# Weights, forms and normed operands placed earlier in the program in the four full units of a two-layer FP32 trunk

## The chip, the cores and the metric

The kernel runs on one core of one Trainium2 chip, as a single launch. The time is device microseconds (us) from the first to the last instruction as the chip measures it for an execution. Engines are named as the profile names them: PE is TensorE (matmuls; PEld are its weight loads), DVE is VectorE, ACT is ScalarE, POOL is GpSimd, SP is SyncE, which here does little but issue the loads.

## The reference

One inference step of a two-layer trunk with model width 1024, all in FP32. 512 columns are a new stream's prompt and 8 x 16 columns are the next frames of eight running streams, so T = 640 columns in all. Each layer has a mixer (layer 0: a gated MLP beside a gated short convolution; layer 1: forgetting attention) and then a convolutional feed-forward network (FFN), both with a residual:

```python
def _rmsnorm(x, g):
    xf = x.astype(jnp.float32)
    y = xf * lax.rsqrt(jnp.mean(xf * xf, axis=-1, keepdims=True) + EPS)
    return (y * g.astype(jnp.float32)).astype(x.dtype)
...
def _conv_ffn(x, prev, w_up, conv_w, w_down):
    z, st = _causal_dwconv(x @ w_up, conv_w, prev)
    gate, up = jnp.split(z, 2, axis=-1)
    return (jax.nn.silu(gate) * up) @ w_down, st
...
        hp = _rmsnorm(xp, norm_ffn[layer])
        hs = _rmsnorm(xs, norm_ffn[layer])
        zero_f = jnp.zeros((xp.shape[0], CONV_W - 1, 2 * D_FF), xp.dtype)
        yp, st_p = _conv_ffn(hp, zero_f, w_up[layer], conv_ffn[layer], w_down[layer])
        ys, st_s = _conv_ffn(hs, state_ffn[layer], w_up[layer], conv_ffn[layer], w_down[layer])
```

The up-projection goes from 1024 to 5632 channels, half of them gate and half up, and the down-projection from 2816 back to 1024. The last two up-projected columns of each stream are returned too (the new state of the convolution).

## The kernel before

**Tiles and precision.** The activations stand transposed, as eight tiles of 128 channels x 640 columns. TensorE multiplies a rounded FP32 form (fp32r), so each operand is split in a high and a low part and a product is the sum of three: high x high, high x low, low x high. A block of 128 output channels over 1024 inputs is 8 x 3 x 2 = 48 matmuls, each of a 128 x 128 weight tile with 320 columns (`mm`, L251). Splitting a 128 x 1024 weight block costs an ACT cast for the high part (`whi`) and then either a DVE subtract for the low part (`wlo`, function `weights`, L94 and L95), or, in `weights_added`, an ACT cast (L102), an ACT negation (L103) and a DMA that POOL issues and that adds the weights from memory onto the negated high part (L104). All loads of weights (`raw`) are issued by SP.

**The FFN.** The 5632 up-projected channels are 22 gate blocks and 22 up blocks. Gate block j and up block j make a unit. A unit's two blocks in PSUM are multiplied by the RMS factor of their columns (`rb`) into an SBUF tile with room for the convolution's history (`pad_evac`: DVE L340 and L341, and a small POOL copy L333). Then come the copy of the new state (ACT, L352), the convolution (ACT L346, DVE L348) of both blocks, SiLU (ACT L495), the product (DVE L498 and L499) and its split for the down-projection (ACT L135, DVE L136). The code calls what follows the eviction `act`.

**Full units and pair units.** Units 0 to 3 are full units: three products for each tile, with weights from `weights` in units 0 and 1 and from `weights_added` in units 2 and 3. From unit 4 on a unit is computed as a pair, gate and up over two halves of the rows and of the columns, by a scheme with seven products in place of eight (`pair_blocks`, matmuls on L201). It needs other operands:

- `forms(p)` makes, from channel tiles 2p and 2p+1 of x, two normed tiles `y` (DVE L152) and three sums and differences of their halves (DVE L156 to L159, 128 x 320 each), and splits these three (a cast and a subtract of 128 x 960, L135 and L136).
- `settle(p)` splits the normed tiles `y` into the tiles `hh` and `hl` in which the full units' operands stood (per tile an ACT cast and a DVE subtract of 128 x 640). It overwrites what the full units read.
- `pair_weights` loads both weight blocks, splits the gate block as it is (first part, up to its `yield`), then forms sums of the quarters (DVE L180) and splits these (second part).

From unit 4 on the down-projections of the four units before stand among the pair's products (`downs`; weights by `weights_down`, whose low part is again an adding DMA of POOL, `wlo<-w_dn`).

**What sets the order.** The program is written in Python and a scheduler of the framework arranges the instructions of each engine by its own estimate of times, with the order of the program as priority; once arranged, an engine runs its instructions strictly in that order. So where a call stands in the program decides which instruction gets in line first, and an instruction that waits holds up those behind it on its engine. Buffers limit how far ahead a weight can be prepared: four `raw` buffers (which the forms' sums use as well), five each of `whi` and `wlo`, eight pairs in the ring that holds the units' products and the forms' tiles `y`, and in PSUM three places of 128 x 1024 for the blocks, used in turn.

In the loop of `ffn` before the change, a unit is written as: load and split its weights and multiply (for unit 1 to 3 block by block), evict, copy the state, convolve and multiply, and last `forms(j)` for one pair of channel tiles. The next unit's weights come after all of this; and in unit 4 come, in this order, its weights' first part, a pair of down-projection weights, its weights' second part, `settle` for all four pairs, and the products.

Of the kernel before, what the change touches and what calls it, by code (L numbers as in the profile page):

```python
# [23 lines left out]
NJ = 22  # L24
PARTS = ((0, 4), (4, 8), (8, 12), (12, 16), (16, 20), (20, 22))
NSTD = 4
# [27 lines left out]
class Core:  # L54
# [28 lines left out]
    def weights(self, src, cols=1024, pieces=1, between=None):  # L83
        nc = self.nc
        raw = self.raw()
        hi = self.wp.tile([P, 1024], F32R, tag="whi", name=self.nm("whi"))
        lo = self.wp.tile([P, 1024], F32R, tag="wlo", name=self.nm("wlo"))
        n = cols // pieces
        for i in range(pieces):
            c = slice(i * n, i * n + n)  # L90
            if i == 1:
                between()
            nc.sync.dma_start(out=raw[:, c], in_=src[:, c])
            nc.scalar.copy(out=hi[:, c], in_=raw[:, c])  # L94
            nc.vector.tensor_tensor(out=lo[:, c], in0=raw[:, c], in1=hi[:, c].bitcast(F32), op=ALU.subtract)  # L95
        return hi, lo
# [36 lines left out]
    def part(self, hi, lo, src):  # L133
        nc = self.nc
        nc.scalar.copy(out=hi, in_=src)  # L135
        nc.vector.tensor_tensor(out=lo, in0=src, in1=hi.bitcast(F32), op=ALU.subtract)  # L136
# [345 lines left out]
    def ffn(self, l, x, h, g, rb, ring, fb, finish, out=None):  # L482


        nc, io = self.nc, self.io
        rpool, rtags = ring
        two = lambda a, n: a.rearrange("p (u c) -> p u c", u=2)

        def act(zg, zu, b):
            cvs = []  # L490
            for z, i in ((zu, 1), (zg, 0)):
                o = O_CF + (l * NB + b + i * NJ) * 3
                cv = self.conv(z, self.cst[:, o:o + 3])
                if i == 0:
                    nc.scalar.activation(out=cv[:, 0:CW], in_=cv[:, 0:CW], func=AF.Silu)  # L495
                cvs.append(self.conv_compact(cv))
            pr = self.tmp()
            nc.vector.tensor_tensor(out=pr[:, 0:TP], in0=cvs[1][0], in1=cvs[0][0], op=ALU.mult)  # L498
            nc.vector.tensor_tensor(out=pr[:, TP:T].rearrange("p (s c) -> p s c", c=16), in0=cvs[1][1], in1=cvs[0][1], op=ALU.mult)  # L499
            return self.split(rpool, rtags, pr[:, :T])  # L500

        def down(n, acts, ob, w):
            a, b = PARTS[n]
            ps = self.psum_d()
            for kc in range(b - a):
                self.mm((ps[:, C0:512], ps[:, 512:512 + HT]), w, kc, acts[kc], kc == 0, kc == b - a - 1)
            self.add_x(x[ob], ps)

        def downs(n, acts, ob):

            a, b = PARTS[n]
            w = self.weights_down(io["w_dn"][l, ob:ob + 2][:, :, a * P:b * P], (b - a) * P)
            return [lambda i=i: down(n, acts, ob + i, w[i]) for i in range(2)]

        forms, f, prev = [], None, None
        hk = [h[c] for c in KORD]
        first = [KORD.index(c) for c in range(NC)]
        zi = 0
        for n, (a, b) in enumerate(PARTS):
            si = self.fx.tile([P, 2, 64], F32, tag="si", name=self.nm("si"), bufs=2)  # L520
            so = self.fx.tile([P, 2, 72], F32, tag="so", name=self.nm("so"), bufs=2)
            nc.scalar.dma_start(out=si[:, :, 0:16 * (b - a)], in_=two(io["st_f"][l], NB)[:, :, 16 * a:16 * b])
            acts, left = [], [0, 2, 4, 6] if n else []
            for j in range(a, b):
                zg, zu = self.zp[zi % 3], self.zp[(zi + 1) % 3]
                zi += 2
                sts = [si[:, i, 16 * (j - a):16 * (j - a) + 16] for i in range(2)]
                if j < NSTD:
                    blocks = (j, NJ + j)
                    if j == 0:  # L530
                        ps = self.blocks([self.weights(io["w_up"][l, i]) for i in blocks], hk, first)
                    else:
                        weights = self.weights if j == 1 else self.weights_added
                        ps = [self.blocks([weights(io["w_up"][l, i])], hk)[0] for i in blocks]
                    for z, p_, st in zip((zg, zu), ps, sts):
                        self.pad_evac(z, p_[:, C0:C0 + T], rb, st)
                else:
                    w = self.pair_weights(io["w_up"][l, j], io["w_up"][l, NJ + j])
                    next(w)
                    dn = downs(n - 1, prev, left.pop(0))  # L540
                    w = next(w)
                    if f is None:
                        f = [self.settle(p, (h[2 * p], h[2 * p + 1]), forms[p]) for p in range(4)]
                    self.pair_blocks(w, f, zg, zu, sts, dn)
                for i, z in enumerate((zg, zu)):
                    self.new_state(z, so[:, i, 18 * (j - a):18 * (j - a) + 18])
                acts.append(act(zg, zu, j))
                if j < NSTD:
                    forms.append(self.forms(j, x, g, rb, ring, fb))
            for ob in left:  # L550
                for d in downs(n - 1, prev, ob):
                    d()
            nc.scalar.dma_start(out=two(io["o_sf"][l], NB)[:, :, 18 * a:18 * b], in_=so[:, :, 0:18 * (b - a)])
            prev = acts
        self.project([io["w_dn"][l, ob][:, a * P:b * P] for ob in range(8)], prev, None, x, finish, cols=(b - a) * P, out=out)
# [532 lines left out]
```

## Time and profile before

| | |
|---|---|
| median of 3 runs | 1645.4 us (1641.4, 1645.4, 1646.24) |
| profiled execution | 1644.36 us |
| its span, first to last instruction | 1642.6 us |
| mean granted TensorE clock | 0.949 |
| PE busy | 1485.1 us, 90% |
| DVE busy | 1055.4 us, 64% |
| ACT busy | 740.1 us, 45% |
| POOL busy | 207.8 us, 13% |

In a view of groups or of one engine's timeline, a row such as `L348 DVE SCALAR_TENSOR_TENSOR t<-zp,cst,t` is line 348 of the kernel on DVE, which writes tile `t` from tiles `zp`, `cst` and `t`; `x4` is the number of instructions in the row, and what stands in brackets is the idle time ahead of it with what ended that. The chain of waits lists, in order of time, start and duration of each piece of work that the next one waited for. The view of windows gives, for stretches of the span, the busy time of each engine with its number of instructions, the granted clock of TensorE (1.00 is full speed) and the share of DMA time. The part of the FFN from unit 0's last eviction to the first product of unit 4 lies at 229 to 349 us in layer 0 and at 1136 to 1256 us in layer 1.

### The profile page before, as it was taken

How to read it: one execution, taken by the hardware profiler on the slowest of the kernel's cores; microseconds unless marked ns; L12 is line 12 of the kernel's file. 1: busy time of each engine (PE TensorE's matmuls, PEld its weight loads, DVE VectorE, ACT ScalarE, POOL GpSimd, SP SyncE). 2: the span in 40 equal slices, each digit the busy share in tenths (PEclk: the TensorE clock that was granted, in tenths of full speed). 3: DMA queues.
4: the chain of work that ended last, by engine and by line, in shares of the span. 5: the costliest groups of instructions: out<-in, count | busy, mean ns of one | idle time of the engine just before them, and what ended most of it. 6: DMA issues, size and time to landing. Idle time of an engine off the chain costs nothing.

```text
span 1642.6 us, 26334 instructions
## 1 busy us (share of the span) xinstructions
PE 1485.1 (90%) x10576; PEld 1431.1 (87%) x10576; DVE 1055.4 (64%) x1805; ACT 740.1 (45%) x1326; POOL 207.8 (13%) x235
## 2 busy tenths in 40 slices
PE   8999965469999999999999999996546999999998
PEld 6999965459999999999989888886546999999998
DVE  6545442277777777677666667567327777877764
ACT  6322321255555555555544444344215555555551
POOL 4100210000101010126101010003000010101010
PEclk9999986779999999999999999998767999999999
DMA  7222102234444454443534424320223444544442
GB/s 249 84 78 65 39 21 60 66 92 103 114 110 121 103 126 103 98 160 111 173 110 133 133 87 170 91 76 26 77 66 88 107 107 105 129 105 120 103 95 87
DMA packets 74249, 168.04 MB, mean 102 GB/s; under 512 B 13760, under 2 KB 22896, under 8 KB 74000
## 3 DMA queue, kind: packets, MB, share of 16 engines
q1 hardware_dynamic: 49392, 133.79, 25.7%
q0 software_dynamic: 12032, 25.17, 9.5%
q10 hardware_dynamic: 12704, 7.41, 1.5%
q8 instruction: 83, 1.36, 0.4%
q14 instruction: 38, 0.31, 0.1%
HBM read 150.58 MB, written 11.54 MB: 99 GB/s over the span
## 4 chain that ended last, share of the span: by engine, by line
PE 86%; DVE 7%; DMA 2%; ACT 2%; issue 2%; POOL 0%; SPq 0%; DVEq 0%; ACTq 0%; POOLq 0%
PE mm L251 36%; PE zx L201 19%; PE pj L690 10%; PE aux L201 8%; PE po L251 2%; PE pv L766 2%; DMA wlo<-w_up 2%; DVE t L348 2%; PE pt L759 1%; DVE hl L282 1%; PE mm L389 1%; DVE wlo L95 1%; PE pt L845 1%; PE sc L752 1%; DVE y L152 1%
## 5 line engine op out<-in xcount | busy, mean ns | idle before, releaser
L135 ACT CAST sh<-raw 128x1024 fp32r<-128x1024 f32 (+2 forms) x152 | 142.4, 944 | 204.5 <-PE zx L201 101.9
L201 PE MATMUL zx<-hh,sh 128*128 128x320 f32 x576 | 179.9, 312 | 25.8 <-ACT sh L135 25.8
L251 PE MATMUL mm<-sh,wlo 128*128 128x320 f32 x872 | 201.4, 308 | 2.0 <-DMA wlo<-w_dn 2.0
L251 PE MATMUL mm<-sh,whi 128*128 128x320 f32 x872 | 200.6, 310 | 1.4 <-DVE x L359 0.9
L251 PE MATMUL mm<-hh,whi 128*128 128x320 f32 x512 | 125.6, 328 | 81.2 <-ACT whi L102 54.1
L251 PE MATMUL mm<-sl,whi 128*128 128x320 f32 x872 | 198.8, 309 | 0.0
L136 DVE TENSOR_TENSOR sl<-raw,sh 128x1024 fp32r<-128x1024 f32 (+2 forms) x152 | 164.8, 1092 | 38.9 <-ACT sh L135 32.7
L348 DVE SCALAR_TENSOR_TENSOR t<-zp,cst,t 128x656 f32<-128x656 f32 x184 | 162.9, 897 | 33.0 <-ACT t L346 31.9
L201 PE MATMUL zx<-hh,sl 128*128 128x320 f32 x576 | 179.0, 312 | 1.6 <-DVE sl L136 1.6
L201 PE MATMUL zx<-hl,sh 128*128 128x320 f32 x576 | 179.5, 312 | 0.0
L251 PEld LDWEIGHTS mm<-hh,whi 128*128 128x128 f32 x512 | 91.9, 202 | 82.9 <-ACT whi L102 55.2
L251 PEld LDWEIGHTS mm<-sh,whi 128*128 128x128 f32 x872 | 146.2, 188 | 2.8 <-DVE x L359 1.8
L251 PEld LDWEIGHTS mm<-sh,wlo 128*128 128x128 f32 x872 | 146.3, 188 | 2.6 <-DMA wlo<-w_dn 2.6
L251 PEld LDWEIGHTS mm<-sl,whi 128*128 128x128 f32 x872 | 146.1, 188 | 0.0
L251 PE MATMUL mm<-hh,wlo 128*128 128x320 f32 x512 | 120.5, 319 | 26.2 <-DMA wlo<-w_up 26.2
L94 ACT CAST whi<-raw 128x1024 fp32r<-128x1024 f32 (+3 forms) x94 | 79.9, 856 | 141.6 <-PE mm L251 85.8
L690 PE MATMUL pj<-whi,hl 128*128 128x256 f32 x480 | 137.3, 287 | 3.1 <-DVE hl L282 3.1
L359 DVE TENSOR_TENSOR x<-mm,x 128x640 f32<-128x640 f32 x111 | 91.2, 822 | 72.9 <-PE mm L251 72.6
L690 PE MATMUL pj<-wlo,hh 128*128 128x256 f32 x480 | 137.2, 286 | 0.0
L690 PE MATMUL pj<-whi,hh 128*128 128x256 f32 x480 | 136.7, 287 | 0.0
L201 PEld LDWEIGHTS zx<-hh,sh 128*128 128x128 f32 x576 | 109.9, 191 | 26.3 <-ACT sh L135 26.3
L251 PE MATMUL mm<-hl,whi 128*128 128x320 f32 x512 | 123.5, 324 | 0.3 <-DVE hl L282 0.3
(232 smaller groups left out, 3374.0 us busy)
## 6 DMA issues: line engine op xcount, KB each, us to landing
raw<-w_up SPq DMA_DIRECT2D x88, 512.0 KB
raw<-w_dn SPq DMA_DIRECT2D x40, 512.0 KB
wlo<-w_dn POOLq DMA_DIRECT2D x40, 512.0 KB, 5.9
raw<-w_c SPq DMA_DIRECT2D x24, 512.0 KB
raw<-w_ab SPq DMA_DIRECT2D x16, 512.0 KB
ck<-c_k SPq DMA_DIRECT2D x16, 512.0 KB
cv<-c_v SPq DMA_DIRECT2D x16, 512.0 KB
o_kv<-z ACTq DMA_DIRECT2D x8, 640.0 KB
```

The lines of the kernel that those rows point to most:

```text
L94: nc.scalar.copy(out=hi[:, c], in_=raw[:, c])
L95: nc.vector.tensor_tensor(out=lo[:, c], in0=raw[:, c], in1=hi[:, c].bitcast(F32), op=ALU.subtract)
L135: nc.scalar.copy(out=hi, in_=src)
L136: nc.vector.tensor_tensor(out=lo, in0=src, in1=hi.bitcast(F32), op=ALU.subtract)
L152: stt(out=y, in0=x[c], scalar=self.gv[:, 8 * g + c:8 * g + c + 1], in1=rb, op0=ALU.mult, op1=ALU.mult)
L201: nc.tensor.matmul(out, lhsT=l[:, c], rhs=r, start=start and p == 0 and i == 0, stop=p == 3 and i == 2, skip_group_check=True)
L251: nc.tensor.matmul(outs[h], lhsT=l, rhs=r[:, h * HT:(h + 1) * HT], start=start and k == 0, stop=stop and k == 2)
L282: nc.vector.scalar_tensor_tensor(out=lo, in0=x, scalar=gs, in1=hi.bitcast(F32), op0=ALU.mult, op1=ALU.subtract)
L348: nc.vector.scalar_tensor_tensor(out=cv[:, 0:CW], in0=zp[:, i:i + CW], scalar=w[:, i:i + 1], in1=cv[:, 0:CW], op0=ALU.mult, op1=ALU.add)
L359: self.nc.vector.tensor_tensor(out=x, in0=ps[:, C0:C0 + T], in1=x, op=ALU.add)
L690: nc.tensor.matmul(out[tb], lhsT=l[:, tb * P:(tb + 1) * P], rhs=r[:, c:c + 256], start=kc == 0 and i == 0, stop=kc == 7 and i == 2)
L766: nc.tensor.matmul(ov[64 * hh:64 * hh + 64, i * P:n], lhsT=z[2][:, j, (2 * pair + hh) * 64:(2 * pair + hh) * 64 + 64], rhs=u[:, j * P:(j + ...
```

## The change

In `ffn` the weights of unit j + 1 are now asked for right after the matmuls of unit j and ahead of its eviction, state copy and `act`; unit 0's are asked for ahead of the loop. In unit 3 the same place holds the first part of unit 4's pair weights and all four `settle`; the second part follows unit 3's evictions and stands ahead of its state copies. Unit 4's first pair of down-projection weights comes after that. The forms of pairs 0 and 1 now stand behind unit 0 and those of pairs 2 and 3 behind unit 1, where before each of the units 0 to 3 had one. The operations are the same as before; loads, casts, subtracts and adding DMAs move with the functions that contain them.

```diff
+        full = lambda j: [(self.weights if j < 2 else self.weights_added)(io["w_up"][l, i]) for i in (j, NJ + j)]
+        part = lambda j: self.pair_weights(io["w_up"][l, j], io["w_up"][l, NJ + j])
+        w = full(0)
         for n, (a, b) in enumerate(PARTS):
...
                 if j < NSTD:
-                    blocks = (j, NJ + j)
-                    if j == 0:
-                        ps = self.blocks([self.weights(io["w_up"][l, i]) for i in blocks], hk, first)
-                    else:
-                        weights = self.weights if j == 1 else self.weights_added
-                        ps = [self.blocks([weights(io["w_up"][l, i])], hk)[0] for i in blocks]
+                    ps = self.blocks(w, hk, first) if j == 0 else [self.blocks([v], hk)[0] for v in w]
+
+                    w = full(j + 1) if j + 1 < NSTD else part(j + 1)
+                    if j + 1 == NSTD:
+                        next(w)
+                        f = [self.settle(p, (h[2 * p], h[2 * p + 1]), forms[p]) for p in range(4)]
                     for z, p_, st in zip((zg, zu), ps, sts):
                         self.pad_evac(z, p_[:, C0:C0 + T], rb, st)
+                    if j + 1 == NSTD:
+                        w = next(w)
                 else:
-                    w = self.pair_weights(io["w_up"][l, j], io["w_up"][l, NJ + j])
-                    next(w)
-                    dn = downs(n - 1, prev, left.pop(0))
-                    w = next(w)
-                    if f is None:
-                        f = [self.settle(p, (h[2 * p], h[2 * p + 1]), forms[p]) for p in range(4)]
+                    if j == NSTD:
+                        dn = downs(n - 1, prev, left.pop(0))
+                    else:
+                        w = part(j)
+                        next(w)
+                        dn = downs(n - 1, prev, left.pop(0))
+                        w = next(w)
                     self.pair_blocks(w, f, zg, zu, sts, dn)
                 for i, z in enumerate((zg, zu)):
                     self.new_state(z, so[:, i, 18 * (j - a):18 * (j - a) + 18])
                 acts.append(act(zg, zu, j))
-                if j < NSTD:
-                    forms.append(self.forms(j, x, g, rb, ring, fb))
+                if j < 2:
+                    forms += [self.forms(p, x, g, rb, ring, fb) for p in (2 * j, 2 * j + 1)]
```

How this moves ACT's instructions is seen in layer 0, from unit 1's state copies on. Before, the rows are these; `sh` of 128 x 640 is the product of unit 1, `sh` of 128 x 960 the forms of pair 1, and the four rows at the end belong to unit 2's weights:

```order
L352 COPY so_2004<-zp_90 128x18
L352 COPY so_2004<-zp_88 128x18
L346 ACTIVATE t_2271<-zp_88,cst 128x656
L346 ACTIVATE t_2275<-zp_90,cst 128x656
L495 ACTIVATE t_2275<-t_2275 128x656
L135 CAST sh_2283<-t_2280 128x640
L135 CAST sh_2296<-raw_2291 128x960
L102 CAST whi_2302<-raw_2300 128x1024
L102 CAST whi_2358<-raw_2356 128x1024
L103 ACTIVATE wlo_2303<-whi_2302 128x1024
L103 ACTIVATE wlo_2359<-whi_2358 128x1024
```

In the changed kernel the same place has these; `whi_2278` to `wlo_2286` are unit 2's weights, and `sh_2161` and `sh_2174` the forms of pairs 0 and 1:

```order
L352 COPY so_2016<-zp_90 128x18
L102 CAST whi_2278<-raw_2276 128x1024
L352 COPY so_2016<-zp_88 128x18
L346 ACTIVATE t_2298<-zp_88,cst 128x656
L346 ACTIVATE t_2302<-zp_90,cst 128x656
L135 CAST sh_2161<-raw_2156 128x960
L103 ACTIVATE wlo_2279<-whi_2278 128x1024
L135 CAST sh_2174<-raw_2169 128x960
L102 CAST whi_2285<-raw_2283 128x1024
L103 ACTIVATE wlo_2286<-whi_2285 128x1024
L495 ACTIVATE t_2302<-t_2302 128x656
L135 CAST sh_2310<-t_2307 128x640
```

Unit 2's first cast went from behind unit 1's SiLU and product to between its state copies, and both negations now stand ahead of the SiLU, behind the conversion of pair 0's forms.

On DVE, the rows from unit 1's second eviction on, in the changed kernel, hold the end of the forms of pairs 0 and 1, interleaved, and then unit 1's convolution:

```order
L340 TENSOR_TENSOR zp_88<-mm_2227,rb_1974 128x512
L158 SCALAR_TENSOR_TENSOR raw_2156<-y_2153,y_2152 128x320
L341 TENSOR_TENSOR zp_88<-mm_2227,rb_1974 128x8x16
L158 SCALAR_TENSOR_TENSOR raw_2169<-y_2166,y_2165 128x320
L159 SCALAR_TENSOR_TENSOR raw_2156<-raw_2156,y_2153 128x320
L159 SCALAR_TENSOR_TENSOR raw_2169<-raw_2169,y_2166 128x320
L348 SCALAR_TENSOR_TENSOR t_2298<-zp_88,cst,t_2298 128x656
L348 SCALAR_TENSOR_TENSOR t_2302<-zp_90,cst,t_2302 128x656
```

Unit 1's subtracts for its low parts (L95), which stood behind unit 0's forms, are no longer ahead of this place on DVE: they went into the stretch before the FFN. In layer 1 that stretch reads on DVE as follows; L359 adds the mixer's output to x, L282 makes the normed low operands, and the two L95 rows are unit 1's:

```order
L359 TENSOR_TENSOR x_80<-mm_11657,x_80 128x640
L95 TENSOR_TENSOR wlo_11869<-raw_11867,whi_11868 128x1024
L95 TENSOR_TENSOR wlo_11875<-raw_11873,whi_11874 128x1024
L282 SCALAR_TENSOR_TENSOR hl_11645<-x_79,gv,hh_11644 128x640
L359 TENSOR_TENSOR x_81<-mm_11696,x_81 128x640
```

Before, the L282 row of `x_79` stood right behind the L359 row of `x_80`, with nothing between them.

## The prediction

> **What bounds the kernel now.** I read the slices of the page first, to see where PE is not full, then the waits of PE, then the windows of the stage in question, and last the chain of waits and the timelines of ACT and DVE inside it.
>
> ```profile
> PE   8999965469999999999999999996546999999998
> PEclk9999986779999999999999999998767999999999
> ```
>
> There are two dips, slices 6 to 8 and 28 to 30, one for each layer's full units, and the granted clock falls with them. PE's waits by releaser:
>
> ```profile
> PE mm L251 <- ACT whi L102: 54.1, 4, 13.5
> PE mm L251 <- ACT whi L94: 27.1, 2, 13.5
> PE mm L251 <- DMA wlo<-w_up: 26.2, 4, 7.7
> PE zx L201 <- ACT sh L135: 25.8, 2, 12.9
> ```
>
> (Total, times, longest, in us.) Together 133.2 us, 66.6 per layer: PE waits three times for the high part of the next unit's first weights (L94 for unit 1, L102 for units 2 and 3), after that in units 2 and 3 for the low part, and once for the operands of the first pair. Nothing else in the list is above 6 us. The windows from unit 0's last eviction to unit 4's first product, layer 0 and layer 1, and two stretches behind the first (duration, then busy time and instructions of PE, PEld, DVE, ACT, POOL, clock, DMA share, GB/s):
>
> ```profile
> 229.24:349.09 119.85, 53.11 (x290) 51.12 (x291) 53.76 (x82) 35.04 (x49) 7.97 (x15) 0.68 0.20 50
> 1136.22:1256.11 119.89, 51.88 (x291) 49.89 (x291) 53.77 (x82) 35.03 (x49) 7.31 (x12) 0.70 0.19 50
> 352.00:400.00 48.00, 45.99 (x307) 45.74 (x306) 35.80 (x51) 25.82 (x40) 4.66 (x6) 0.98 0.53 141
> 400.00:700.00 300.00, 300.00 (x2049) 300.00 (x2049) 222.21 (x321) 161.25 (x263) 33.32 (x47) 1.00 0.45 110
> ```
>
> In 119.85 us no engine is busy even half of the time, so this stage is bound by the chain through the engines. The last row gives the price of a matmul at full rate, 300.00/2049 = 0.146 us; a block (48) costs 7.05, a unit 14.1, and units 1 to 3 need 42.3 of the 119.85. The timeline of ACT shows the chain of one unit:
>
> ```profile
> 260.69 1.57 ACT L346 ACTIVATE t<-zp,cst 128x656 f32<-128x656 f32 x2
> 264.94 0.75 ACT L495 ACTIVATE t<-t 128x656 f32<-128x656 f32 x1 [2.67 <-DVE t L348]
> 266.65 0.72 ACT L135 CAST sh<-t 128x640 fp32r<-128x640 f32 x1 [0.96 <-DVE t L499]
> 271.16 0.99 ACT L135 CAST sh<-raw 128x960 fp32r<-128x960 f32 x1 [3.79 <-DVE raw L159]
> 272.06 1.99 ACT L102 CAST whi<-raw 128x1024 fp32r<-128x1024 f32 x2
> 273.95 2.00 ACT L103 ACTIVATE wlo<-whi 128x1024 fp32r<-128x1024 f32 x2
> ```
>
> Unit 2's cast at 272.06 needs only a loaded weight, but stands behind unit 1's convolution, SiLU, product and forms.
>
> **The change part by part.** Times t below count from 229.24, layer 0. DVE there, unit 0:
>
> ```profile
> 229.24 0.69 DVE L340 TENSOR_TENSOR zp<-mm,rb 128x512 f32<-128x512 f32 x1
> 229.85 0.28 DVE L341 TENSOR_TENSOR zp<-mm,rb 128x128 f32<-128x128 f32 x1
> 231.15 3.34 DVE L348 SCALAR_TENSOR_TENSOR t<-zp,cst,t 128x656 f32<-128x656 f32 x4 [1.02 <-ACT t L346]
> 235.91 0.28 DVE L499 TENSOR_TENSOR t<-t,t 128x128 f32<-128x128 f32 x1
> 236.99 0.83 DVE L136 TENSOR_TENSOR sl<-t,sh 128x640 fp32r<-128x640 f32 x1
> 237.73 0.88 DVE L152 SCALAR_TENSOR_TENSOR y<-x,gv,rb 128x640 f32<-128x640 f32 x1
> 238.64 0.49 DVE L156 TENSOR_TENSOR raw<-y,y 128x320 f32<-128x320 f32 x1
> 239.17 0.49 DVE L157 TENSOR_TENSOR y<-y 128x320 f32<-128x320 f32 x1
> 241.77 1.16 DVE L136 TENSOR_TENSOR sl<-raw,sh 128x960 fp32r<-128x960 f32 x1 [1.06 <-ACT sh L135]
> 242.84 2.35 DVE L95 TENSOR_TENSOR wlo<-raw,whi 128x1024 fp32r<-128x1024 f32 x2
> ```
>
> From start to start these give 0.9 for an eviction, 0.8 for an L152 or a 640 subtract, 0.52 for each of L156 to L159, 1.07 for a 960 subtract, 1.18 for an L95. The rows behind are the low-part DMAs on the chain of waits (start, duration), layer 0 and then 1, and the matmuls that follow the first:
>
> ```profile
> 275.34 5.66 DMA wlo<-w_up
> 312.11 7.39 DMA wlo<-w_up
> 1181.20 6.34 DMA wlo<-w_up
> 1217.75 7.99 DMA wlo<-w_up
> 281.05 15.39 PE mm L251 x88
> ```
>
> The mean landing is 6.85, and 88 matmuls after a pause cost 15.4 where full rate asks 12.9: 2.5 are the slow clock.
>
> *Unit 1.* Its weights are cast and subtracted ahead of the FFN, so PE runs from t 0 to 14.1. DVE ends unit 0's product at 6.95 (235.91 + 0.28 - 229.24), evicts unit 1's first block to 7.8, makes four L152 and a subtract (4.0) and four of the 0.52 us rows (2.1) to 13.9, and then evicts the second block, which is there at 14.1, to 15.0. Four more short rows end the two forms at 17.1.
>
> *Unit 2.* In ACT's new order `sh_2161` and then `wlo_2279` stand behind the two L346 (0.2 for L352 and 1.57: to 16.8). `sh_2161` ends at 17.7, `wlo_2279` at 18.6, its DMA lands at 25.5. Its `whi` is cast before that, so PE, after eight more matmuls (15.3), has one wait of about 10 here in place of two. The 88 matmuls that are then left end at 40.9.
>
> *Unit 3.* DVE goes on from 17.1: convolution 3.35 and two 960 subtracts 2.1 (22.6), SiLU 0.75 and product 0.9 (24.3), four L152 and a subtract (28.3), eight short rows (32.5). ACT converts both forms (34.5), then `wlo_2441` (35.4), which lands at 42.3; PE needs it four matmuls after 40.9, at 41.5, so about 0.8 is lost. New wait: the second block's cast `whi_2447` is queued behind L352, which waits for unit 2's first eviction, near 35; its low part lands at about 45 and is needed only at 48.6. Unit 3 ends at 56.0.
>
> *Pair start.* DVE's order puts unit 3's second eviction ahead of five of the eight settling subtracts, two other subtracts and an L180; from 56.0 these take 0.9 + 5 x 0.8 + 0.7 + 1.2 + 0.7 = 7.5, and the last operand is there at 63.5.
>
> ```profile
> L136 DVE TENSOR_TENSOR sl<-raw,sh 128x512 fp32r<-128x512 f32 x36 | 24.8, 690 | 18.9 <-ACT sh L135 12.9 <-PE aux L201 6.0
> L136 DVE TENSOR_TENSOR sl<-raw,sh 128x1024 fp32r<-128x1024 f32 x108 | 131.1, 1221 | 13.7 <-ACT sh L135 13.5
> wlo<-w_dn POOLq DMA_DIRECT2D x40, 512.0 KB, 5.9
> ```
>
> PE has about 54 products of ready operands among them, 54 x 0.146 = 7.9, so it can stay nearly covered, but the down-projection weights' accumulate (5.9 median) is now issued only behind the settling casts. I take 6 lost here in place of the 2.0 that row 352 to 400 shows lost (48.00 - 45.99), net 4; the bounds are 0 (all covered) and 9, nearly the last wait in the list above, 12.9 less some 4 of the settling that now comes early. The interval is then 56.0 + 4 = 60.0 and the gain 119.85 - 60.0 = 59.8. In layer 1 both of unit 2's casts stand behind the two L346, which adds two casts (2.0): 57.8.
>
> *Lead-in.* In layer 0 unit 1's weights go into a stretch with PE continuous and room on DVE. In layer 1 two L95 are put ahead of the L282 for which PE waits at the end of that stretch. Beside the adds of POOL they last longer than the 1.18 above:
>
> ```profile
> 1111.09 1.86 DVE L95 TENSOR_TENSOR wlo<-raw,whi 128x1024 fp32r<-128x1024 f32 x1
> 1114.99 2.59 DVE L95 TENSOR_TENSOR wlo<-raw,whi 128x1024 fp32r<-128x1024 f32 x1
> 1112.36 4.15 POOL L289 TENSOR_TENSOR acc<-acc,t 128x640 f32<-128x640 f32 x2 [0.48 <-ACT t L288]
> ```
>
> Two cost 2.4 to 5.2, or 0 where a wait for a matmul hides them; I take 3. The Trainium skill, page "SBUF — State Buffer", section "Who interferes with whom", says that a DVE instruction which reads two SBUF operands and a GpSimd instruction contend for one port, and that the loser stands fully blocked rather than slowed. The rows above agree in direction: 1.86 and 2.59 beside the adds. By that rule alone the pair could lose two whole adds on top of its own work, 2.4 + 4.15 = 6.5, and the sum would be 3.5 longer; the measured rows decide here.
>
> *Sum.* 59.8 + 57.8 - 3 = 114.6 against the profiled execution: 1644.4 - 114.6 = 1529.8. The median of the runs is 1.0 above that execution, so 1531.
>
> **The rivals.**
>
> *Waits vanish more fully, about 1509.* If unit 2's wait is halved (5 per layer, the forms done earlier) and the pair starts without a loss (6 per layer), 22 more are saved. For it: engines half idle in the window. Against: the low part of unit 2 is still behind one form and a DMA of 6.85. If PE never waited, 119.85 - 42.3 = 77.5 per layer would go, and 1489 is the floor.
>
> *DVE and DMAs slower, about 1557.* The window packs 54 us of DVE work into 60, with the DMAs of L104 among it:
>
> ```profile
> DMA to landing us min/median/max: 5.7/7.9/9.4
> ```
>
> If each of the four on the chain lands at the maximum, 9.4 in place of 6.85 (+10 in all), the pair start stays as dear as the 12.9 shown (7 above my 6, two layers: +14), and the lead-in costs 5.2 (+2), 26 come on top. For it: loads, forms and settling now coincide; against: the DMA share there was 0.20 and doubles to about 0.4 in half the time, less than the 0.53 of the row behind it.
>
> *The change does not do what it says, about 1645.* If the arranger had left unit 2's casts behind unit 1's forms and product, the chain above would stand. The order of ACT shown with the change speaks against it; in layer 1 the casts are behind the L346 alone.
>
> *Slower, about 1675.* The arranger plans the whole program anew. If its new order in the pair stage lets PE wait in each pair, as no wait does now (300.00 busy of 300.00), then with 36 pairs (the x36 row: one 512 split for each) the gain is gone at 114.6/36 = 3.2 us a pair; with 4 a pair, 144 are lost and the time is 1531 + 144 = 1675. For it: DVE is already at 222.21 of 300 there, and a subtract behind a late product would stall all. Against: no pair's code but the first is changed, and rows of the same kinds run in it.
>
> **How the numbers follow.** The forecast, 1512 to 1546, has 0.66; waits vanish more fully 0.12; slower DVE and DMAs 0.17; no effect 0.02; slower 0.03. The range 1504 to 1567 takes in the bounds: downward 8 for the pair starts, 3 for the lead-in and most of the second case; upward 10 for the pair starts, 2 for the lead-in, and the third case with some 10 beyond its time. A measurement of this kernel can tell about 0.3%, 4.9 us, from no change; by the cases, faster 0.95, the same 0.02, slower 0.03.
>
> **What would show it.** In the profile after, the two dips are shorter: the interval from unit 0's last eviction to the first L201 is 56 to 60 (layer 0), not 120. The waits for `whi` on L94 and L102 are nearly gone, those for `wlo<-w_up` come to 10 or 13 in unit 2 and under 2 in unit 3, and that for `sh` L135 is below 6 per layer. The lead-in of layer 1 grows by 2 to 5. If unit 2 begins much later than t 25, my reading of the queue on ACT is wrong; if the pair stage no longer shows PE at 300 of 300, the slower case is there.

## The result, and the profile after

The changed kernel takes 1528.5 us in the median (four runs, 1525.8 to 1532.7) against 1645.2 of the kernel before, a ratio of 0.930 (95% interval 0.927 to 0.932). That is 2.5 us below the forecast of 1531 and inside its narrower range. The profiled execution took 1525.84 us, with a span of 1524.0; the spans differ by 118.6 us where the sum had 114.6.

In the page of the changed kernel, the busy times and the slices of PE and of the granted clock show what is left of the two dips:

```profile
PE 1471.2 (97%) x10576; PEld 1418.3 (93%) x10576; DVE 1047.9 (69%) x1805; ACT 736.9 (48%) x1326; POOL 211.1 (14%) x235
...
PE   8999997899999999999999999999699999999998
...
PEclk9999998999999999999999999999899999999999
```

The number of instructions is that of before on every engine (10576, 1805, 1326, 235), and the busy times are within 14 us of it. What is gone is idle time. PE's waits by releaser, changed kernel:

```profile
PE mm L251 <- DMA wlo<-w_up: 10.9, 2, 8.0
PE mm L251 <- ACT whi L102: 10.4, 3, 6.2
...
PE mm L251 <- DMA wlo<-w_dn: 2.8, 1, 2.8
PE mm L251 <- DVE hl L282: 2.0, 1, 2.0
...
PE zx L201 <- ACT sh L135: 1.3, 1, 1.3
```

The four rows that stood for 133.2 us come to 22.6: L94 has left the list, L102 went from 54.1 to 10.4, the low parts from 26.2 to 10.9, and the first pair's operands from 25.8 to 1.3. The windows from unit 0's last eviction to the first of an unbroken row of pair products (layer 0, layer 1; busy times in the order PE, PEld, DVE, ACT, POOL, then clock, DMA share, GB/s), and then the longer stretch of layer 0 in which PE issues the 606 recorded matmuls that the stretch below it holds of the kernel before:

```profile
229.52:284.00 54.48, 45.41 (x288) 44.74 (x287) 44.40 (x71) 28.57 (x39) 9.62 (x13) 0.87 0.43 110
1075.76:1133.60 57.84, 45.67 (x283) 44.61 (x282) 45.63 (x74) 29.66 (x42) 8.26 (x10) 0.85 0.46 112
229.52:338.90 109.38, 94.92 (x606) 92.78 (x605) 87.91 (x134) 59.62 (x89) 15.51 (x22) 0.92 0.43 108
```

```profile
229.24:400.00 170.76, 102.02 (x606) 99.76 (x607) 92.40 (x135) 63.23 (x91) 12.75 (x21) 0.76 0.30 76
```

The interval fell from 119.85 to 54.48 us in layer 0 and from 119.89 to 57.84 in layer 1, that is by 65.4 and 62.1. Over the longer stretch layer 0 gains 170.76 - 109.38 = 61.4, so 4.0 of the 65.4 are given back when the pairs start. Counted from unit 0's last eviction to the start of attention's projections, 726.6 - 229.24 = 497.4 before and 665.5 - 229.52 = 436.0 after, the gain is 61.4 as well.

Inside unit 2 of layer 0, the matmuls of the changed kernel that waited, and the rows of ACT that they waited for:

```profile
250.33 0.90 PE L251 MATMUL mm<-hh,whi 128*128 128x320 f32 x2 [6.18 <-ACT whi L102]
254.66 0.90 PE L251 MATMUL mm<-hh,wlo 128*128 128x320 f32 x2 [2.90 <-DMA wlo<-w_up]
```

```profile
237.60 1.05 ACT L102 CAST whi<-raw 128x1024 fp32r<-128x1024 f32 x1
244.93 0.21 ACT L352 COPY so<-zp 128x18 f32<-128x18 f32 x1 [6.28 <-DVE zp L341]
245.04 1.57 ACT L346 ACTIVATE t<-zp,cst 128x656 f32<-128x656 f32 x2
246.52 0.98 ACT L135 CAST sh<-raw 128x960 fp32r<-128x960 f32 x1
247.40 1.05 ACT L103 ACTIVATE wlo<-whi 128x1024 fp32r<-128x1024 f32 x1
248.36 0.97 ACT L135 CAST sh<-raw 128x960 fp32r<-128x960 f32 x1
249.24 1.04 ACT L102 CAST whi<-raw 128x1024 fp32r<-128x1024 f32 x1
```

The first cast is done at 238.6. Its negation needs nothing else, but stands in line behind a state copy for which ACT idles 6.28 us, behind the convolution and behind pair 0's forms. So the wait in unit 2 is still one of order.

### The profile page after: what moved, and what is told of

Read it like the earlier page. It is cut to its first block, busy times and chain, and to the rows that moved or that the text cites. A ratio compares the mean times of both kernels' runs of the same rounds, so it can differ in the third digit from the quotient of the medians.

```text
span 1524.0 us, 26325 instructions
## 1 busy us (share of the span) xinstructions
PE 1471.2 (97%) x10576; PEld 1418.3 (93%) x10576; DVE 1047.9 (69%) x1805; ACT 736.9 (48%) x1326; POOL 211.1 (14%) x235
## 3 DMA queue, kind: packets, MB, share of 16 engines
q0 software_dynamic: 12032, 25.17, 10.4%
## 4 chain that ended last, share of the span: by engine, by line
PE 90%; DVE 3%; issue 2%; DMA 2%; ACT 2%; SPq 0%; POOL 0%; DVEq 0%; POOLq 0%
PE mm L251 37%; PE zx L201 20%; PE pj L696 11%; PE aux L201 8%; PE pv L772 3%; PE po L251 2%; PE pt L765 1%; DVE hl L282 1%; PE mm L389 1%; DVE wlo L95 1%; DMA wlo<-w_up 1%; PE pt L851 1%; PE sc L758 1%; PE sc L759 1%; PE scs L830 1%
## 5 line engine op out<-in xcount | busy, mean ns | idle before, releaser
L94 ACT CAST whi<-raw 128x1024 fp32r<-128x1024 f32 (+3 forms) x94 | 80.1, 856 | 149.6 <-PE mm L251 85.8
L359 DVE TENSOR_TENSOR x<-mm,x 128x640 f32<-128x640 f32 x111 | 91.2, 822 | 69.3 <-PE mm L251 69.0
L251 PE MATMUL mm<-hh,whi 128*128 128x320 f32 x512 | 120.3, 317 | 10.4 <-ACT whi L102 10.4
L251 PE MATMUL mm<-hh,wlo 128*128 128x320 f32 x512 | 118.5, 314 | 10.9 <-DMA wlo<-w_up 10.9
L251 PE MATMUL mm<-hl,whi 128*128 128x320 f32 x512 | 119.4, 315 | 2.0 <-DVE hl L282 2.0
L95 DVE TENSOR_TENSOR wlo<-raw,whi 128x1024 fp32r<-128x1024 f32 (+3 forms) x94 | 101.6, 1084 | 23.5 <-ACT whi L94 23.3
```

The source lines that it names most:

```text
L251: nc.tensor.matmul(outs[h], lhsT=l, rhs=r[:, h * HT:(h + 1) * HT], start=start and k == 0, stop=stop and k == 2)
L359: self.nc.vector.tensor_tensor(out=x, in0=ps[:, C0:C0 + T], in1=x, op=ALU.add)
```

## The experiments

The times are medians; the ratio is to the kernel before on the same chip. The changed kernel was run a second time beside the second group, with 1527.6 us, ratio 0.9281 (0.9266 to 0.9297).

| kernel | us | ratio, 95% interval |
|---|---|---|
| weights alone | 1549.2 | 0.9419 (0.9405 to 0.9434) |
| forms alone | 1574.0 | 0.9577 (0.9563 to 0.9591) |
| all but the pair's part | 1528.5 | 0.9297 (0.9280 to 0.9313) |
| subtract for the low parts of units 2 and 3 | 1516.3 | 0.9226 (0.9209 to 0.9242) |
| weights two units ahead | 1509.8 | 0.9171 (0.9157 to 0.9186) |
| both of these | 1510.1 | 0.9177 (0.9161 to 0.9193) |
| unit 1's low parts by DMA | 1523.9 | 0.9259 (0.9244 to 0.9273) |
| two ahead, one tap less | 1503.0 | 0.9146 (0.9133 to 0.9158) |
| two ahead, unit 1 by DMA | 1504.3 | 0.9156 (0.9143 to 0.9168) |

### The weights' part alone

```diff
-                    w = full(j + 1) if j + 1 < NSTD else part(j + 1)
-                    if j + 1 == NSTD:
-                        next(w)
-                        f = [self.settle(p, (h[2 * p], h[2 * p + 1]), forms[p]) for p in range(4)]
+                    w = full(j + 1) if j + 1 < NSTD else None
...
-                if j < 2:
-                    forms += [self.forms(p, x, g, rb, ring, fb) for p in (2 * j, 2 * j + 1)]
+                if j < NSTD:
+                    forms.append(self.forms(j, x, g, rb, ring, fb))
```

(Against the changed kernel; unit 4 is again as in the kernel before.)

> The weights' part of the change alone: the next full unit's weights ahead of a unit's evictions; forms again one pair behind each of units 0 to 3, unit 4's weights and the settling where they stood before. Theory (what kept PE waiting was the place of the next unit's casts behind the unit's chain and forms; the forms only matter in so far as they stand in unit 3 just ahead of the first pair): units 1 to 3 run as in the changed kernel, unit 2's low part lands at t 25 to 26 and unit 3 ends near t 55, but then the last form and the settling are all still to come and the pair waits about 13 us for sh (L135) as in the kernel before. Interval 55 + 14 = 69 in place of 119.85, gain 2 x 51 - 1 = 101: 1544 us (1536 to 1552). Rival (the weights are all of it, the forms cost nothing at the pair's start): 1528. Rival (two forms per unit are what shortens the chain, the weights follow from it): above 1590.

Measured: 1549.2, inside the theory's range and far from both rivals. PE's waits of this kernel:

```profile
PE zx L201 <- ACT sh L135: 28.9, 2, 14.4
PE mm L251 <- DMA wlo<-w_up: 12.2, 2, 6.3
PE mm L251 <- ACT whi L102: 5.7, 4, 2.4
```

The waits for weights are as short as in the changed kernel, 17.9 us, but the pair's wait for its operands is not shortened at all: 28.9, against 25.8 before. So the weights' place alone gives 1643.8 - 1549.2 = 95 us (against the kernel before on this chip), and most of what it leaves over is the pair's start.

### The forms' part alone

```diff
-                if j < NSTD:
-                    forms.append(self.forms(j, x, g, rb, ring, fb))
+                if j < 2:
+                    forms += [self.forms(p, x, g, rb, ring, fb) for p in (2 * j, 2 * j + 1)]
```

(Against the kernel before.)

> The forms' part alone: the kernel before with two pairs of forms behind unit 0 and two behind unit 1, none behind units 2 and 3; all weights where they stood before. Theory: units 1 and 2 still wait for casts behind the chain, now with two forms in it (some 3 us more each), but no form is left between unit 2 and unit 3 and between unit 3 and the pair: ACT's order has unit 3's casts right behind unit 2's, so unit 3's wait (13.5 + about 6) goes, and the pair's start loses about 8 less. Per layer 20 + 8 + 5 - 6 = 27 to 35, so 1575 to 1592 us. Rival (only the weights' place matters): 1640 to 1650. Rival (the forms are all of it): 1530.

Measured: 1574.0, a gain of 70 and 1 us past the better end of the theory's range. The matmuls of layer 0 that waited in this kernel, from unit 0 to the pair:

```profile
239.88 0.90 PE L251 MATMUL mm<-hh,whi 128*128 128x320 f32 x2 [8.75 <-ACT whi L94]
246.45 0.90 PE L251 MATMUL mm<-hh,wlo 128*128 128x320 f32 x2 [5.13 <-DVE wlo L95]
271.26 0.90 PE L251 MATMUL mm<-hh,whi 128*128 128x320 f32 x2 [8.75 <-ACT whi L102]
280.09 0.90 PE L251 MATMUL mm<-hh,whi 128*128 128x320 f32 x2 [7.40 <-ACT whi L102]
289.34 0.90 PE L251 MATMUL mm<-hh,wlo 128*128 128x320 f32 x2 [6.74 <-DMA wlo<-w_up]
```

Two waits for unit 1, three for unit 2, none for unit 3 and none for the pair's products: with no form behind unit 2, unit 3's casts stand right behind unit 2's, as expected. The two parts give 95 and 70 us alone and 117 together, so they overlap by 48. Unit 3's waits go with either of them and can go only once; in the kernel before they were 13.53 and 7.09 us in layer 0 and 13.53 and 7.70 in layer 1, which is 42 of the 48. Where the rest of the overlap lies stays open.

### The pair's part undone

```diff
-                    w = full(j + 1) if j + 1 < NSTD else part(j + 1)
-                    if j + 1 == NSTD:
-                        next(w)
-                        f = [self.settle(p, (h[2 * p], h[2 * p + 1]), forms[p]) for p in range(4)]
+                    w = full(j + 1) if j + 1 < NSTD else None
```

(Unit 4 is again as in the kernel before; weights and forms as in the changed kernel.)

> The changed kernel with the pair's part undone: weights early and forms two per unit, but the first pair's weights and the settling asked for in unit 4, behind the first down-projection weights, as before. The recorded step counted the earlier settling as a help at the pair's start (6 us lost there per layer where before it was 12.9). If that is right, undoing it costs up to 7 per layer: 1535 to 1542 us. Rival: the settling can start no earlier than the last read of the operands by unit 3 wherever it stands in the program, and the order of ACT and DVE hardly differs, except that the negation for wlo<-w_dn comes ahead of the settling again: then the wait for wlo<-w_dn (2.8 us in layer 0 of the changed kernel) goes, and it is 2 to 6 us faster than the changed kernel, 1523 to 1527.

Measured: 1528.5, the time of the changed kernel to 0.1 us. The help that the prediction saw in the earlier settling isn't there, and the 2 to 6 us of the rival aren't either. The rival's mechanism can be seen: the wait for `wlo<-w_dn` is no longer in the list of this kernel, but others have come in its place.

```profile
PE mm L251 <- ACT sh L135: 3.8, 3, 3.2
PE zx L201 <- DVE zp L341: 3.3, 2, 2.3
```

So at the pair's start it was the forms' move that helped, as it took two forms from behind units 2 and 3: the kernel with the weights alone differs from this one in the forms only, takes 1549.2, and waits 28.9 us there. Where the settling and the pair's weights stand in the program is worth nothing that these runs can tell.

### The low parts of units 2 and 3 by a subtract

```diff
-        full = lambda j: [(self.weights if j < 2 else self.weights_added)(io["w_up"][l, i]) for i in (j, NJ + j)]
+        full = lambda j: [self.weights(io["w_up"][l, i]) for i in (j, NJ + j)]
```

> The changed kernel with units 2 and 3 using the cast and DVE subtract of units 0 and 1 for their low parts in place of negation and adding DMA. Theory (what is left in unit 2 is the landing of the adding DMA, 5.8 in layer 0 and 8.2 in layer 1, behind the forms on ACT): the low part is there 1.2 us after DVE reaches it, right behind the forms, so the wait for wlo (2.9 in layer 0, 8.0 in layer 1) goes; but the second block's high part, for which PE waits first (6.2 in layer 0), stays behind the forms, and DVE has four subtracts of 1.2 more per layer. Net 5 to 9 us faster than the changed kernel: 1520 to 1524. Rival (DVE is the bound of this stage once PE's waits are short: 9.4 us more work on it show in full): 1536 to 1540.

Measured: 1516.3, 12 us faster than the changed kernel. The direction is the theory's, the size is not. In layer 0 one wait is left in unit 2:

```profile
247.24 0.90 PE L251 MATMUL mm<-hh,wlo 128*128 128x320 f32 x2 [3.13 <-DVE wlo L95]
```

The expectation kept the 6.18 us for the second block's high part. In layer 0 it is gone as well: by the order of PE's rows, the arranger now lets PE finish the first block before it turns to the second, where in the changed kernel it had interleaved the two, and PE stopped at a cast that it did not need yet. In layer 1 the wait of 7.98 for the low part is gone, and two waits for high parts are left, 3.63 and 0.80. The rival, that DVE's 9.4 us of added work would show, is out.

### Weights two units ahead

```diff
-        w = full(0)
+        ahead = [full(0), full(1)]
...
+                    w = ahead.pop(0)
                     ps = self.blocks(w, hk, first) if j == 0 else [self.blocks([v], hk)[0] for v in w]
-                    w = full(j + 1) if j + 1 < NSTD else part(j + 1)
+                    if j + 2 < NSTD:
+                        ahead.append(full(j + 2))
+                    if j + 1 == NSTD:
+                        w = part(j + 1)
```

(Beside it, on the same chip, the changed kernel once more.)

> The changed kernel unaltered, beside the three below on one chip, so that differences of a few us can be read: 1525 to 1532 us. No theory says otherwise.

> The changed kernel with the weights of the full units asked for two units ahead in place of one: units 0 and 1 ahead of the loop, unit 2's behind unit 0's matmuls, unit 3's behind unit 1's. In the arranged program all of unit 2's casts and negations come ahead of unit 0's evictions, so PE's wait in unit 2 (9.1 us in layer 0, 12.2 in layer 1) must go. Theory (with weights early, DVE is next: its work from unit 0's last eviction to the last settling subtract, laid end to end, was about 60 us in the working of the prediction, and PE has 42.3): the full units end near t 43 to 45, the saved time comes back in part as a wait of the first pairs for settled operands, and 3 to 8 us per layer are left: 1513 to 1523 us. Rival (DVE keeps up, PE's waits in unit 2 are simply gone): 1505 to 1508. Rival (the order's place of casts is not what holds unit 2): 1528.

Measured: 1527.6 for the changed kernel and 1509.8 for this one, 17.8 us faster; a little better than the theory's range and above the rival's. Its windows from unit 0's last eviction, layer 0 for the full units alone and then with the first pair:

```profile
229.68:273.90 44.22, 44.11 (x300) 43.62 (x298) 40.89 (x68) 24.98 (x38) 7.61 (x12) 1.00 0.37 88
229.68:290.00 60.32, 55.50 (x353) 54.26 (x352) 56.96 (x91) 35.20 (x53) 13.08 (x15) 0.92 0.38 100
```

The full units run without a gap, 44.11 of 44.22 us at clock 1.00, and the waits are behind them, at the pair:

```profile
275.27 0.41 PE L201 MATMUL zx<-hh,sh 128*128 128x320 f32 x1 [1.34 <-ACT sn L216]
277.05 0.63 PE L201 MATMUL zx<-hl,sh 128*128 128x320 f32 x1 [0.84 <-DVE hl L136]
282.61 0.63 PE L201 MATMUL aux<-sh,sl 128*128 128x320 f32 x1 [2.54 <-DVE sl L136]
```

DVE is busy 56.96 us of 60.32 here. That makes it the next bound by its busy time; whether its work sets the time is tried below, by taking some of it away.

### Two ahead and the subtract

The edits of the two last experiments together.

> As the run before (weights two units ahead), and the low parts of units 2 and 3 by a DVE subtract in place of negation and adding DMA. The subtract alone made the changed kernel 12 us faster, by taking away the DMA's landing. With the weights two units ahead that landing is hidden, and if DVE is the bound then, four subtracts of 1.2 us per layer, of which unit 2's two fall before the stage, cost 2 to 5 per layer: 4 to 10 us slower than the run before. Rival (the gains of the two edits add): 12 us faster than the run before.

Measured: 1510.1, the same as two units ahead alone. The gains do not add, which fits that both edits remove the same wait, that of unit 2. The loss of 4 to 10 us that the added subtracts were to cost does not show in the medians; the spans of the two profiled executions, 1509.5 and 1506.1, are 3.4 apart in its direction. So if there is a cost, it is at the low end or below what was expected, and the runs do not settle it.

### Two ahead and one tap less

```diff
-                cv = self.conv(z, self.cst[:, o:o + 3])
+                cv = self.conv(z, self.cst[:, o:o + 3], (1,) if b < NSTD else (1, 0))
```

(Against the kernel with weights two units ahead; `conv` is given the list of its DVE taps. This kernel leaves out a part of the convolution in the full units, so it returns other values and serves to measure only.)

> The kernel with weights two units ahead, with one of the two DVE taps of the convolution left out in the four full units (their convolutions have two taps in place of three; nothing else is left out). That takes two DVE instructions of 0.84 us from each unit, 6.7 us per layer, 5.0 of them ahead of the settling. Theory (with weights two ahead DVE is the bound: 56.96 us busy of the 60.32 from unit 0's last eviction on, in layer 0): 4 to 6 us per layer, 1498 to 1502 us. Rival (what is left at the first pair is the latency of the chain through ACT, POOL and DMAs, or the share of it that DVE sets is small): 1506 to 1510.

Measured: 1503.0, 1 us outside the theory's range and 3 from the rival's. By the ratios, 0.9146 against 0.9171, it gains 4 us, half of the least that the theory asked for the two layers together; the spans of the profiled executions are 7.5 us apart (1506.1 and 1498.6). From unit 0's last eviction to the start of attention's projections layer 0 gains 4.6 (657.7 - 229.68 = 428.0, and 652.3 - 228.88 = 423.4), nearly all of the 5.0 us of DVE work that was taken from ahead of the settling, so there the time follows DVE's work. Layer 1 gains only 2 us of 5. At its first pair PE's waits for DVE become shorter (2.66 to 1.18 for `sl`), but its wait for the cast `sh` grows from 2.26 to 3.42, and that cast stands on ACT behind the load of its weight; a wait of 1.71 for a down-projection weight comes in too. So DVE as the bound is shown for layer 0, by one profiled execution of each kernel, and not for layer 1.

### Unit 1's low parts by DMA

```diff
-        full = lambda j: [(self.weights if j < 2 else self.weights_added)(io["w_up"][l, i]) for i in (j, NJ + j)]
+        full = lambda j: [(self.weights if j < 1 else self.weights_added)(io["w_up"][l, i]) for i in (j, NJ + j)]
```

> The changed kernel with unit 1's low parts by negation and adding DMA in place of DVE's subtract, so that no subtract of unit 1 is ahead of the FFN on DVE any more. In the changed kernel the two subtracts took 4.48 us of DVE there in layer 1 and PE waited 2.0 for the next normed operand. Theory (the step of the prediction that charged 3 us for the lead-in, bounds 0 to 5.2, was too dear, since the next stop, the adds on POOL, is hardly later): 0.5 to 2 us faster than the changed kernel. Rival (blocked DVE time shows in full, as by the 6.5 us worked out beside the page): 4 to 6.5 us faster.

Measured: 1523.9, 3.7 us faster, between the two expectations. In the changed kernel DVE's lead-in of layer 1 reads

```profile
1057.22 0.81 DVE L359 TENSOR_TENSOR x<-mm,x 128x640 f32<-128x640 f32 x1
1057.95 4.56 DVE L95 TENSOR_TENSOR wlo<-raw,whi 128x1024 fp32r<-128x1024 f32 x2
1062.44 0.87 DVE L282 SCALAR_TENSOR_TENSOR hl<-x,gv,hh 128x640 fp32r<-128x640 f32 x1
```

and unit 0's evictions there began at 1075.15, without the two subtracts at 1072.80:

```profile
1075.15 1.29 DVE L340 TENSOR_TENSOR zp<-mm,rb 128x512 f32<-128x512 f32 x2 [3.83 <-ACT rb L325]
```

```profile
1072.80 1.29 DVE L340 TENSOR_TENSOR zp<-mm,rb 128x512 f32<-128x512 f32 x2 [3.83 <-ACT rb L325]
```

The first and last start of attention's first group of projections are the same in both, 665.5 and 951.3 in the changed kernel and 665.6 and 951.3 without the subtracts:

```profile
L696 PE MATMUL pj<-whi,hh x480: 277/283/387, 665.5 to 951.3; 128*128 128x256 f32 x160
```

```profile
L696 PE MATMUL pj<-whi,hh x480: 277/283/387, 665.6 to 951.3; 128*128 128x256 f32 x160
```

So the two cost 2.35 us of time for 4.56 of DVE. What the medians show beyond that, 1.3 us, is less than the spread of the runs. With the weights two units ahead, the same edit gives the fastest complete kernel of this study:

> The kernel with weights two units ahead, and unit 1's low parts by negation and adding DMA. Both edits alone made the changed kernel faster, by 18 and by 3.7 us. The second one acts ahead of the FFN of layer 1 (unit 0's evictions come 2.35 us earlier there), where the first one has changed nothing, so the gains should add: 1505 to 1508 us. Rival (four adding DMAs of 512 KB ahead of the stage in place of two arrive late, and unit 1 or 2 waits for them): 1510 to 1516.

Measured: 1504.3, just below the theory's range. The ratio is 0.9156 against 0.9171 with the subtracts, which is 2.5 us of the 3.7 that the edit gave alone, and the two intervals overlap. Of the profiled difference of 4.6 us, 3.2 come from ahead of layer 1's evictions. So the direction is that of gains that add, the size is not settled, and the rival's late DMAs did not come.

## Why the prediction was right, point by point

**The bound.** It was right that PE waited for casts that stood in line, and that the stage holds 42 us of PE work. Moving the weights alone brings 95 us.

**Unit 2.** The low part was to land at t 25.5 in layer 0 and 27.5 in layer 1. In the chain of waits of the changed kernel the two adding DMAs are

```profile
248.79 5.83 DMA wlo<-w_up
...
1095.43 8.16 DMA wlo<-w_up
```

and end at 254.62 - 229.52 = 25.1 and 1103.59 - 1075.76 = 27.8. The chain on ACT and DVE was laid end to end from single rows of the kernel before, and that held to within 1 us, since each engine runs its rows in the order shown. That the landings agree to 0.4 us is luck in part: the DMAs started at t 19.3 and 19.7, where 18.6 and 20.6 were worked out, and took 5.83 and 8.16, where the mean of 6.85 stood for both, so in each layer one error makes up for the other. What failed is a detail: PE was to do eight matmuls and then wait once for about 10 us. It did four, waited 6.18 for the second block's cast, which the order on ACT showed behind both forms, and then 2.90 for the low part: 9.1 in all.

**Unit 3.** 0.8 us were charged for its low part, and no wait is there. The second block's cast behind the state copy was a new wait in the program and cost nothing, as worked out.

**Pair start.** A net loss of 4 per layer was taken between bounds of 0 and 9: 4.0 in layer 0, and about the same in layer 1 (62.1 less the 58.1 gained there from unit 0's last eviction to the end: 118.6 - (1136.22 - 1075.76) = 58.1). In layer 0 the cause is the one named: PE waits 1.27 us for a cast and then 2.81 for the accumulate of the down-projection weights, whose negation stands behind settling casts. In layer 1 PE waits 3.08 at the same place. The number was right and one of its reasons was not: the prediction let the earlier settling help, and the kernel without it is as fast.

**Lead-in.** 3 us were charged, with bounds of 0 and 5.2. Against the kernel before, unit 0's last eviction came 0.6 us later, counted from the start of attention's projections (in the kernel before they start at 726.6: 1136.22 - 726.6 = 409.6, and 1075.76 - 665.5 = 410.3). The two subtracts do cost 2.35, as their removal shows, so the rest of the lead-in became 1.7 shorter; where that comes from stays open. The price of the two rows was at the lower end of the 2.4 to 5.2 worked out, and as a difference between the kernels the term was mis-sized.

**The sum.** Predicted 59.8 + 57.8 - 3 = 114.6, measured 61.4 + 58.1 - 0.6 - 0.3 = 118.6, where the last 0.3 is a later start of layer 0's stage. The lead-in is the largest difference. Layer 0's interval came out shorter than the sign of 56 to 60 said, 54.48. Two slips of the working do not bear on the result: 48 matmuls at 300.00/2049 are 7.03 us, not 7.05, and the floor of 1489 lacks the 1.0 that was added to the forecast for the median.

**The rivals.** Slower DMAs did not cost time: the two that PE waited for took 5.83 and 8.16 us, between 5.7 and 9.4. All eight landed a little later than before (median 8.3 after 7.9, at most 10.2), but PE did not wait for the other six. The case in which more of the waits vanish did not come with this change, as unit 2's wait of 9 to 12 us per layer stayed; asking for the weights two units ahead takes that wait away and reaches 1510. That the case had 1509 is chance, since it halved unit 2's wait and let the pair start without a loss, while here the whole wait is gone and the pair still waits. The slower case, a pair stage that stalls in each pair, is out: in the changed kernel PE is busy for 298.70 of 300.00 us in the pair stage, and in the kernel before for 300.00 of 300.00.

```profile
300.00:600.00 300.00, 298.70 (x2034) 297.88 (x2034) 224.73 (x324) 161.74 (x261) 29.88 (x46) 1.00 0.45 111
```

## What to carry to other kernels

Where no engine of a stage is busy for half of the time, read the order of the queue, not the busy shares: work that needs only a load, but stands in the program behind the last unit's chain, waits for that chain. Lay the new order end to end with durations of the old trace, engine by engine, with every cast of the other buffers in its place in line, for PE stopped at the one that was left out. When the waits are gone, look for the engine that was nearest to full next (here DVE, 57 of 60 us), and undo the parts one by one: one of the three parts of this change gave nothing.

## What the runs showed of the hardware

Two subtracts of 128 x 1024 on DVE, 1.18 us each elsewhere, took 4.56 us together (2.05 and 2.58 with a small overlap) in the rows of the lead-in shown above, while POOL added in SBUF:

```profile
1057.35 1.57 POOL L289 TENSOR_TENSOR acc<-acc,t 128x640 f32<-128x640 f32 x1 [3.46 <-ACT t L288]
1059.67 1.76 POOL L289 TENSOR_TENSOR acc<-acc,t 128x640 f32<-128x640 f32 x1 [0.75 <-ACT t L288]
```

The two adds end at 1058.92 and 1061.43, and the two subtracts at 1060.00 and 1062.51, each 1.08 us later: about the time that a subtract needs alone. The Trainium skill, page "SBUF — State Buffer", section "Who interferes with whom", has the loser of such a pair fully blocked, and these rows agree with that. The prediction's 6.5 us by this rule was too much because it took two whole adds of 2.08 on top of the subtracts; here the adds were shorter, and each subtract waited only for what was left of one. Of the 4.56 on DVE, only 2.35 reached the time.

A pause of PE costs more than its length. In the kernel before, the 88 matmuls behind a wait took 15.4 us, where the rate of the pair stage (0.146 us each) gives 12.9. With no wait in the full units (two units ahead) the granted clock was 1.00 over units 1 to 3, where the changed kernel had 0.87.
